# A hybrid diffusion layer on one core: GpSimd's tables, weight splits and key copies on VectorE and ScalarE, and a latent scan in 8 blocks of 4 chunks

## The chip, the cores and the metric

The kernel runs on one core of a Trainium2 chip. The time is the device time of one execution in microseconds (us); less is better. Five engines work beside each other, each through its own queue: TensorE (PE) does the matmuls and transposes, VectorE (DVE), ScalarE (ACT) and GpSimd (POOL) the work on elements, and SyncE (SP) issues the loads from HBM.

## The reference

One layer over 256 latent tokens and 256 context tokens of 1024 channels, batch 1, all in float32:

```
mod  = silu(c) @ w_mod + b_mod                      # six rows: shift, scale, gate, twice
h    = rmsnorm(x) * (1 + scale) + shift             # the same for the context tokens
proj = h @ w_in                                     # S5 input 512 | K 128 | V 128 | Q 512 | gates 2048
y    = S5(proj): 32 groups of 16 channels, 64 complex states, both directions;
       the context's last state is the start of the latent scan
o    = attention of the latents over latents and context (8 query heads, 2 key heads,
       normalised q and k, rotary positions on the latents)
x    = x + gate1 * ((gates_a * glu(gelu(y)) @ w_ssm_out + gates_b * o @ w_attn_out) @ w_out)
h2   = rmsnorm(x) * (1 + scale2) + shift2
x    = x + gate2 * sum over the top 4 of 32 experts: swiglu(h2 @ w_gate_up[e]) @ w_down[e]
out  = rmsnorm(x) * final_norm_g
```

## The kernel before

SBUF is used as 24 pages of 128 x 2048 floats (`pg(i)`, L54). A page is filled by a load, read by matmuls, and given back with `release` (L151) or `used` (L172): this issues the next load of one long list (gates, GLU, output projections, then for each expert eight tiles of w_gate_up and four of w_down, 1 MB each). All loads stand in SyncE's queue in program order (`load`, L89), so that a load that waits for its page holds up those behind it.

The work has two parts. The dense part (to about 380 us in the profile) makes the modulation, the projections, S5, attention and the merge. In the experts' part every expert's weights stream through the pages.

A planner orders each engine's instructions by program order and readiness; only where `strict["on"]` is set are TensorE's instructions pinned to program order (L79 to L86). It is off up to the gate splits and on from there. SyncE's loads are always pinned. VectorE, ScalarE and GpSimd are not pinned in the dense part up to the merge.

S5 is worked in chunks of 8 tokens, 32 chunks for the context and 32 for the latents. `v_tables` (L553) builds for each quarter of the groups a real and an imaginary table from the input matrix and powers of the multiplier, six operations on 128 x 1024 floats; of quarters 0 and 1 the imaginary half runs on GpSimd. `v_transposes` (L574) transposes them on TensorE. `w_tables` (L596) builds the readout tables in the same way, six operations for each of four quarters, all on GpSimd, three quarters ahead of the key and value projections and the last after the transposes of U. `scan_multipliers` (L516) fills the tile `LS` with the multiplier's powers for 1, 2, 4, 8 and 16 chunks by 28 operations on 128 x 32 floats. `chunk_in` and `chunk_T` (L727, L739) give each chunk's own contribution to the state, in `vv[0]` (page 8) for the context and `vv[1]` (page 9) for the latents. `scan_up` (L864) reduces the context to one state `h0` in five levels. `scan_steps` (L877) walks over the latents' chunks one after the other: 31 steps of `cmul_add` (L852), which is four VectorE operations, here on 128 x 64 floats.

`split` (L61) takes a float32 weight apart into a rounded part, copied by ScalarE, and the rest, subtracted by the engine that it is given. `gate_split` (L766) does so for the gate columns, two pieces of 512 columns a call, on GpSimd.

After the gate splits of tile 0 and `scan_up` a loop of 16 steps u runs. Each step has 24 gate matmuls (`gate_mm`, L920, which also splits half of the next gate tile), up to u = 8 a part of the scan, up to u = 7 one group of `k_kernel` (L946), which reads all four W tables, and from u = 4 on a step of attention. After u = 7 the kernels go to HBM (`Rd`), and after `scan_out` at u = 9 `kernel_in` (L1041) loads them back in another layout; the readout follows at u = 11 and 12.

Of the kernel before, what the change touches and what calls it, by code (L numbers as in the profile page):

```python
# [15 lines left out]
AF = mybir.ActivationFunctionType  # L16
# [13 lines left out]
P_QT, P_K, P_M, P_A, P_S, P_RO, P_RT, P_GL, P_B, P_BS, P_BL, P_BP = 1, 0, 10, 4, 9, 11, 13, 15, 1, 3, 1, 3  # L30
# [3 lines left out]
def hybrid_block(ctx: ExitStack, tc: tile.TileContext, a: dict, out: bass.AP):  # L34
    nc = tc.nc
    V, S, G, T = nc.vector, nc.scalar, nc.gpsimd, nc.tensor
# [17 lines left out]
    def pg(i, o=0, n=PW):  # L54
        return pages[i][:, o:o + n]
# [5 lines left out]
    def split(src, hi, lo, eng):  # L61
        S.activation(hi.bitcast(F32R), src, AF.Copy)  # L62
        eng.tensor_sub(lo.bitcast(F32R), src, hi)  # L63
# [63 lines left out]
    stream, loaded, where = [], {}, {}  # L127
# [23 lines left out]
    def release(*ps):  # L151
        for p_ in ps:
            renew(p_)
            j = state["next"]
            state["next"] = j + 1
            if j < len(stream):
                key, src = stream[j]
                k, f = src.shape[1], src.shape[2]
                t = pg(p_, 0, k * f).rearrange("p (k f) -> p k f", k=k)
                if j == len(stream) - 1:  # L160
                    for k in (0, 4):
                        load(t[:, k:k + 4], src[:, k:k + 4])
                else:
                    load(t, src)
                loaded[key], where[key] = t, p_
            elif j == len(stream):
                state["fg"] = p_
                fg_row = pg(p_, 1024, 1024)[0:1]
                load(fg_row, a["final_norm_g"][None, :])
                G.partition_broadcast(pg(p_, 0, 1024), fg_row)  # L170
# [39 lines left out]
    wu = [load_cols(w_in, 0, 512, 22, 0, 4)]  # L210
# [302 lines left out]
    LS = sm([128, 5, 2, 2, 32], "LS")  # L513
# [39 lines left out]
    def v_tables(qt):  # L553
        gs = slice(8 * qt, 8 * qt + 8)
        td = pg(7, 0, 1024).rearrange("p (g t k) -> p g t k", g=8, t=8)

        def bc(r):
            return BB[:, r, gs].unsqueeze(2).to_broadcast([128, 8, 8, 16])

        def lc(r):  # L560
            return LV[:, r, :, gs].rearrange("p t g -> p g t").unsqueeze(3).to_broadcast([128, 8, 8, 16])

        VR, VI = v_part(qt, 0), v_part(qt, 1)
        V.tensor_mul(VR, bc(0), lc(0))
        V.tensor_mul(td, bc(1), lc(1))
        V.tensor_sub(VR, VR, td)
        E2 = V
        if qt < 2:
            E2, td = G, pg(20, 0, 1024).rearrange("p (g t k) -> p g t k", g=8, t=8)
        E2.tensor_mul(VI, bc(0), lc(1))  # L570
        E2.tensor_mul(td, bc(1), lc(0))
        E2.tensor_add(VI, VI, td)  # L572

    def v_transposes(qt):  # L574
        for g2 in range(4):
# [18 lines left out]
    WR, WI = [], []  # L594

    def w_tables(qt):  # L596
        gs = slice(8 * qt, 8 * qt + 8)
        td = pg(20, 1024 * (qt % 2), 1024).rearrange("p (g j k) -> p g j k", g=8, j=8)
        for r, tab in ((0, WR), (1, WI)):
            tab.append(pg((18, 19, 11, 12)[qt], 1024 * r, 1024).rearrange("p (g j k) -> p g j k", g=8, j=8))  # L600

        def cc(r):
            return CT[:, r, gs].unsqueeze(2).to_broadcast([128, 8, 8, 16])

        def lw(r):
            return LW[:, r, :, gs].rearrange("p t g -> p g t").unsqueeze(3).to_broadcast([128, 8, 8, 16])

        G.tensor_mul(WR[qt], cc(0), lw(0))
        G.tensor_mul(td, cc(1), lw(1))
        G.tensor_add(WR[qt], WR[qt], td)  # L610
        G.tensor_mul(WI[qt], cc(1), lw(0))
        G.tensor_mul(td, cc(0), lw(1))
        G.tensor_sub(WI[qt], WI[qt], td)

# [23 lines left out]
    renew(11, "r")  # L640
    wuh, wul = [pg(p_).rearrange("p (k f) -> p k f", k=4) for p_ in (12, 11)]
    for k in range(4):
        split(wu[1][:, k], wuh[:, k], wul[:, k], V if k % 2 else G)
    last = mod0_rows(1)
    del held["m", 0], held["m", 1]
    with tc.issue_after(last.ins):
# [17 lines left out]
    mod_tile()  # L664
    renew(11)
    renew(12)
    for qt in range(3):
        w_tables(qt)
    v_transposes(1)
    v_tables(3)  # L670
    v_transposes(2)
# [26 lines left out]
    for h in range(2):  # L698
        for j4 in range(2):
            b = bank()  # L700
# [10 lines left out]
    for h in range(2):  # L711
        for g4 in range(2):
            b = bank()
# [3 lines left out]
            V.tensor_copy(U[:, 4 * g4:4 * g4 + 4, :, h], b.rearrange("p (g q c) -> p g q c", g=4, q=4))  # L717

    mod_tile()
    w_tables(3)  # L720
    split(wq[1], wqh[1], wql[1], V)
    mod_load(16)

# [15 lines left out]
    def chunk_T(i, vo):  # L739
        b = bank()  # L740
        for j in range(2):
            for r in range(2):
                ttrans(b[:, 128 * (2 * r + j):128 * (2 * r + j) + 128],
                            vo[:, 256 * j + 128 * r:256 * j + 128 * r + 128], ident)
        for h in range(2):
            bv = b.rearrange("p (r g h c) -> p h c r g", r=2, g=4, h=2)[:, h]
            V.tensor_copy(vv[h][0:64, :, :, 4 * i:4 * i + 4], bv[0:64])
            S.activation(vv[h][64:128, :, :, 4 * i:4 * i + 4], bv[64:128, ::-1], AF.Copy)

    prev = None  # L750
    for i in range(8):
# [6 lines left out]
        if i in (2, 4):  # L758
            q_proj(i // 2 - 1)
    chunk_T(7, prev)  # L760
    release(20)
    renew(4)

# [2 lines left out]
    def gate_split(i, j):  # L766
        for k in range(0, 8, GK):
            sl = slice(k, k + GK)
            split(loaded["gate", i][:, sl, 128 * j:128 * j + 128], wgh[:, j, sl], wgl_[:, j, sl], G)


    cosq, sinq = sm([128, 2, 64], "cosq"), sm([128, 2, 64], "sinq")
# [40 lines left out]
    for tt in range(4):  # L813
        kvw = kv_ps[tt // 2].rearrange("p (t h f) -> p t h f", t=2, h=4)[:, tt % 2, 0:2]
        r_k = rsn[:, 16 + 2 * tt:18 + 2 * tt]
        d0 = kn[:, tt, :, 0]
        if tt < 2:
            V.tensor_mul(d0, kvw, kg_row.unsqueeze(1).to_broadcast([128, 2, 64]))
            V.tensor_mul(d0, d0, r_k.unsqueeze(2).to_broadcast([128, 2, 64]))
        else:  # L820
            rope_norm(d0, kvw, cosk[:, tt - 2], sink[:, tt - 2], r_k, 2, d0)
        G.tensor_copy(kn[:, tt, :, 1], d0)


    qs = pg(22).rearrange("p (t h r f) -> p t h r f", r=2, t=2, h=8)
# [26 lines left out]
    def cmul_add(h_out, h_in, v_in, lv, n, t1, t2):  # L852
        lr_ = LS[:, lv, 0].unsqueeze(1).to_broadcast([128, n, 2, 32])
        li_ = LS[:, lv, 1].unsqueeze(1).to_broadcast([128, n, 2, 32])
        V.tensor_mul(t1, h_in, lr_)  # L855
        V.tensor_mul(t2, h_in[:, :, ::-1], li_)
        V.tensor_add(t1, t1, v_in)
        V.tensor_add(h_out, t1, t2)  # L858
# [3 lines left out]
    h0 = LS[:, 4, 0:1]  # L862
# [9 lines left out]
            n //= 2  # L872


    H = [h0] + [vv[1][:, s:s + 1] for s in range(31)]

    def scan_steps(s0, s1):  # L877
        for s in range(s0, s1):
            cmul_add(H[s + 1], H[s], H[s + 1], 0, 1, LS[:, 2, 0:1], LS[:, 3, 0:1])

    Hn = pg(8).rearrange("p (g r c) -> p g r c", g=32, r=2)

# [266 lines left out]
    for u in range(16):  # L1149
        gate_mm(u // 2, u % 2)  # L1150
        if mods["done"] < 16:
            p_ = mod_tile()
            if mods["done"] == 16:
                release(23)
        i = u // 2 + 1
        if u % 2 and i < 8 and not (where["gate", i] == 20 and state["next"] >= 8):
            used("gate", i)
        if u == P_QT:
            for i in range(2):
                q_T(i)  # L1160
                k_T(i)
        if P_K <= u < 8 + P_K:
            k_kernel(u - P_K)
        if u == 7 + P_K:
            Rd = dpool.tile([16, 32, 240], F32, name="Rd")
            for q in range(4):
                for e in range(2):
                    load(Rd[:, 8 * q:8 * q + 8].rearrange("p (g e) m -> p e g m", e=2)[:, e],
                                R[32 * q + 16 * e:32 * q + 16 * e + 16].rearrange("p (g e) m -> p e g m", e=2)[:, e])
        if u == P_M:  # L1170
            mod_rows(1)
            mod_rows(2)
        if u == P_M + 1:
            shift_logits()
        if u >= P_A:
            attn(n_attn)
            n_attn += 1
        if u == P_S:
            scan_out()
            kernel_in()  # L1180
        if u < P_S:
            s1 = 31 * (u + 1) // P_S
            scan_steps(n_scan, s1)
            n_scan = s1
        if u in (P_RO, P_RO + 1):
            readout(u - P_RO)
        if u == P_RO + 1:
            release(18, 19, 11, 12, 9)
            load(n2row, w("norm2_g")[None, :].to_broadcast([128, 1024]))
        if u == P_RT:  # L1190
            readout_T()
            gelu()
        if u == 15:
            wsplit()
            wsplit()
        if u == P_GL:
            glu()
        for n in range(3):
            if u == P_B + P_BS * n:
                bias_load(1024 * n, w("b_gate_up")[:, 1024 * n:1024 * n + 1024] if n < 2 else w("b_down"))  # L1200
            for j in range(2):
                if u == P_B + P_BS * n + P_BL + j:
                    bias_parts(1024 * n, (512 * j,))
# [519 lines left out]
```

## Time and profile before

| | us |
|---|---|
| median of 3 runs | 1323.57 |
| lowest and highest | 1322.31 to 1325.38 |
| the profiled execution | 1321.38 |
| its span, first to last instruction | 1319.7 |

In the span TensorE is busy 1170.8 us, VectorE 439.7, ScalarE 196.5 and GpSimd 158.1. 462.57 MB are moved. The rows below name instructions by the line of the kernel (L522), the engine, and out<-in by tile (`pg` is any page, `bk` a PSUM bank).

### The profile page before, as it was taken

Reading aid. Unit: us, or ns where it says so; the run is one execution under the profiler, and the core shown is the slowest. Engines: PE = TensorE matmul, PEld = TensorE weight load, DVE = VectorE, ACT = ScalarE, POOL = GpSimd, SP = SyncE. Lnnn points to the kernel's source line nnn. Section 1 sums busy time; section 2 is a strip of 40 time slices with the busy share of each in tenths; the row PEclk is TensorE's granted clock in tenths of the full one; section 3 lists DMA queues with packets and bytes.
Section 4 is the critical chain, followed back from the end, with each engine's and each line's share of the span. In section 5 each row is a group of like instructions: output and inputs, shape, how many; then the busy total and the mean of one; then the engine's idle time right before and its main releaser. Section 6 shows DMA issues by size and latency. Waiting matters only on the chain.

```text
span 1319.7 us, 16264 instructions
## 1 busy us (share of the span) xinstructions
PE 1170.8 (89%) x6711; PEld 541.5 (41%) x6712; DVE 439.7 (33%) x929; ACT 196.5 (15%) x368; POOL 158.1 (12%) x115
## 2 busy tenths in 40 slices
PE   4563998689999999999999989999898989899986
PEld 2363666578843333333332323323232323233224
DVE  5999389757331121111221111121111111111111
ACT  3231343654110000000000000000000000000001
POOL 1479563412000000000000000000000000000000
PEclk9876899889999999999999999999999999999998
DMA  9810567777989999999999999999999999999996
GB/s 277 279 33 33 191 233 240 116 219 276 352 337 416 416 417 416 416 418 417 418 418 417 418 417 416 417 416 417 417 418 417 417 417 417 417 417 415 416 392 205
DMA packets 123105, 462.57 MB, mean 351 GB/s; under 512 B 20669, under 2 KB 46953, under 8 KB 88210
## 3 DMA queue, kind: packets, MB, share of 16 engines
q1 hardware_dynamic: 122562, 460.90, 89.7%
q8 instruction: 55, 0.90, 0.3%
q0 software_dynamic: 416, 0.56, 0.1%
q14 instruction: 24, 0.20, 0.0%
q10 hardware_dynamic: 48, 0.01, 0.0%
HBM read 459.89 MB, written 1.54 MB: 350 GB/s over the span
## 4 chain that ended last, share of the span: by engine, by line
PE 49%; DMA 37%; DVE 10%; issue 2%; SPq 1%; ACT 1%; POOL 0%; DVEq 0%; ACTq 0%; POOLq 0%
PE bk L83 46%; DMA pg<-in_w_gate_up_dram 28%; DMA pg<-in_w_down_dram 7%; PE bk L86 3%; DMA pg<-Rd 1%; DVE pg L63 1%; DVE pg L858 1%; SPq L90 1%; DVE LS L528 1%; DVE LS L855 1%; DVE pg L522 0%; DVE LS L523 0%; DVE pg L848 0%; DVE pg L380 0%; DVE LS L529 0%
## 5 line engine op out<-in xcount | busy, mean ns | idle before, releaser
L83 PE MATMUL bk<-pg,pg 128*64 128x512 f32 (+6 forms) x5344 | 995.6, 476 | 65.6 <-DMA pg<-in_w_down_dram 28.3
L83 PEld LDWEIGHTS bk<-pg,pg 128*64 128x64 f32 (+3 forms) x5344 | 448.3, 154 | 552.4 <-issue 351.8
L86 PE MATMUL bk<-ident,pg 128*128 128x128 f32 x480 | 83.0, 301 | 57.3 <-DVE pg L572 21.0
L1460 DVE TENSOR_SCALAR pg<-bk 128x512 f32<-128x512 f32 x32 | 22.1, 692 | 290.7 <-PE bk L83 290.7
L1371 DVE TENSOR_TENSOR pg<-bk,shT 128x512 f32<-128x512 f32 x32 | 22.1, 692 | 266.4 <-PE bk L83 266.4
L86 PEld LDWEIGHTS bk<-ident,pg 128*128 128x128 f32 x480 | 56.6, 150 | 123.0 <-issue 48.1
L1577 POOL DMA_DIRECT2D pg<-g2d x2 | 1.3, 642 | 882.2 <-PE bk L83 882.2
L1493 DVE TENSOR_TENSOR pg<-bk,pg 128x512 f32<-128x512 f32 x30 | 20.8, 692 | 188.8 <-PE bk L83 188.8
L1472 ACT ACTIVATE pg<-bk 128x256 f32<-128x256 f32 x32 | 12.3, 383 | 395.4 <-PE bk L86 395.4
L83 PE MATMUL bk<-pg 64*128 64x512 f32 (+1 forms) x368 | 70.5, 486 | 0.0
L1477 ACT ACTIVATE pg<-bk 128x512 f32<-128x512 f32 x32 | 19.1, 596 | 257.4 <-PE bk L86 257.4
L63 POOL TENSOR_TENSOR pg<-pg,pg 128x512 fp32r<-128x512 f32 x34 | 47.5, 1412 | 43.8 <-ACT pg L62 36.8
L62 ACT ACTIVATE pg<-pg 128x512 fp32r<-128x512 f32 (+3 forms) x63 | 43.7, 721 | 56.8 <-PE bk L83 35.8
L1461 ACT ACTIVATE pg<-pg 128x512 f32<-128x512 f32 x32 | 20.1, 630 | 187.0 <-DVE pg L1460 186.9
L83 PEld LDWEIGHTS bk<-pg 64*128 64x128 f32 (+1 forms) x368 | 20.0, 162 | 50.4 <-issue 50.4
L63 DVE TENSOR_TENSOR pg<-pg,pg 128x512 fp32r<-128x512 f32 (+3 forms) x29 | 33.7, 1176 | 3.3 <-ACT pg L62 2.9
L83 PE MATMUL bk<-pg,selB 128*64 128x512 bf16 (+1 forms) x196 | 34.4, 388 | 0.0
L83 PE MATMUL bk<-pg,scond 128*32 128x256 f32 (+1 forms) x256 | 29.0, 525 | 0.0
L1462 DVE TENSOR_SCALAR pg<-bk 128x512 f32<-128x512 f32 x32 | 22.1, 692 | 5.3 <-PE bk L83 5.3
L1463 DVE TENSOR_TENSOR pg<-pg 128x512 f32<-128x512 f32 x32 | 21.8, 683 | 2.1 <-ACT pg L1461 2.0
L1464 DVE SCALAR_TENSOR_TENSOR pg<-pg 128x512 f32<-128x512 f32 x32 | 22.1, 692 | 1.1
L1468 DVE TENSOR_SCALAR pg<-iot,posp,gate 128x128 f32<-128x128 f32 x64 | 18.9, 340 | 0.0
(301 smaller groups left out, 539.1 us busy)
## 6 DMA issues: line engine op xcount, KB each, us to landing
pg<-in_w_gate_up_dram SPq DMA_DIRECT2D x256, 1024.0 KB, 20.0
pg<-in_w_down_dram SPq DMA_DIRECT2D x127, 1024.0 KB, 20.0
pg<-in_w_mod_dram SPq DMA_DIRECT2D x16, 1024.0 KB, 5.4
pg<-in_w_in_dram SPq DMA_DIRECT2D x13, 1024.0 KB, 9.0
pg<-in_w_mod_dram SPq DMA_DIRECT2D x16, 512.0 KB, 9.1
pg<-in_w_out_dram SPq DMA_DIRECT2D x4, 1024.0 KB, 11.8
pg<-Rd SPq DMA_DIRECT2D x16, 128.0 KB, 8.5
pg<-in_w_ssm_out_dram SPq DMA_DIRECT2D x2, 1024.0 KB
```

Source lines behind the costliest of these rows:

```text
L62: S.activation(hi.bitcast(F32R), src, AF.Copy)
L63: eng.tensor_sub(lo.bitcast(F32R), src, hi)
L83: pinned(T.matmul(*ar, **kw))
L86: pinned(T.transpose(*ar))
L1371: pv_(V.tensor_add(xg[p % 2][:, 4 * half:4 * half + 4], pb.rearrange("p (k m) -> p k m", k=4), shk[:, 4 * half:4 * half + 4].unsqueeze(2). ...
L1460: pv_(V.tensor_scalar(gx, pgate, 7.0, None, op0=ALU.min))
L1461: pa_(S.activation(sx, gx, AF.Sigmoid, scale=1.702))
L1462: pv_(V.tensor_scalar(ux, pup, 7.0, -7.0, op0=ALU.min, op1=ALU.max))
L1463: pv_(V.tensor_mul(gx, gx, sx))
L1464: pv_(V.scalar_tensor_tensor(ux, ux, 1.0, gx, op0=ALU.add, op1=ALU.mult))
L1477: pa_(S.activation(dst, pmx, AF.Copy))
L1493: pv_(V.tensor_mul(yx, pdn, g2h))
```

## The change

The GpSimd operations of `v_tables`, `w_tables`, `gate_split` and of the splits of the S5 input's weights go to VectorE; the four copies of the normalised keys go to ScalarE. The four calls of `w_tables` now stand together behind the last `chunk_T`, and their scratch lies in pages 19, 11, 12 and 3 instead of page 20. GpSimd keeps the rotary tables, memsets, broadcasts and a few loads.

The 31 steps over the latents' chunks become 15 pieces. Three pieces combine, for 8 blocks of 4 chunks at once, the chunks of a block into one sum `Sb`; one copy and seven small steps carry the state over the blocks (`Hb`, with the multiplier's power for four chunks, `LS[:, 2]`); three pieces spread it over the chunks of all blocks at once; one copy sets the last chunk of each block. The big pieces are `cmul_add` on 128 x 512 floats.

```diff
@@ v_tables
-        E2 = V
-        if qt < 2:
-            E2, td = G, pg(20, 0, 1024).rearrange("p (g t k) -> p g t k", g=8, t=8)
-        E2.tensor_mul(VI, bc(0), lc(1))
-        E2.tensor_mul(td, bc(1), lc(0))
-        E2.tensor_add(VI, VI, td)
+        V.tensor_mul(VI, bc(0), lc(1))
+        V.tensor_mul(td, bc(1), lc(0))
+        V.tensor_add(VI, VI, td)
@@ w_tables
-        td = pg(20, 1024 * (qt % 2), 1024).rearrange("p (g j k) -> p g j k", g=8, j=8)
+        td = pg((19, 11, 12, 3)[qt], 0, 1024).rearrange("p (g j k) -> p g j k", g=8, j=8)
...
-        G.tensor_mul(WR[qt], cc(0), lw(0))
-        G.tensor_mul(td, cc(1), lw(1))
-        G.tensor_add(WR[qt], WR[qt], td)
-        G.tensor_mul(WI[qt], cc(1), lw(0))
-        G.tensor_mul(td, cc(0), lw(1))
-        G.tensor_sub(WI[qt], WI[qt], td)
+        V.tensor_mul(WR[qt], cc(0), lw(0))
+        V.tensor_mul(td, cc(1), lw(1))
+        V.tensor_add(WR[qt], WR[qt], td)
+        V.tensor_mul(WI[qt], cc(1), lw(0))
+        V.tensor_mul(td, cc(0), lw(1))
+        V.tensor_sub(WI[qt], WI[qt], td)
@@ the projection of the S5 input
-    split(wu[1][:, k], wuh[:, k], wul[:, k], V if k % 2 else G)
+    split(wu[1][:, k], wuh[:, k], wul[:, k], V)
@@ ahead of the key and value projections
-    for qt in range(3):
-        w_tables(qt)
@@ after the transposes of U
-    w_tables(3)
@@ after the chunks
     chunk_T(7, prev)
+    for qt in range(4):
+        w_tables(qt)
     release(20)
@@ gate_split
-            split(loaded["gate", i][:, sl, 128 * j:128 * j + 128], wgh[:, j, sl], wgl_[:, j, sl], G)
+            split(loaded["gate", i][:, sl, 128 * j:128 * j + 128], wgh[:, j, sl], wgl_[:, j, sl], V)
@@ the keys
-        G.tensor_copy(kn[:, tt, :, 1], d0)
+        S.activation(kn[:, tt, :, 1], d0, AF.Copy)
@@ the scan over the latents' chunks
-    H = [h0] + [vv[1][:, s:s + 1] for s in range(31)]
+    vb = vv[1].rearrange("p (b i) r g -> p i b r g", i=4)
+    Sb, Hb, tb1, tb2 = [pg(8, 512 * i, 512).rearrange("p (s r g) -> p s r g", s=8, r=2) for i in range(4)]
+    def scan_pieces():
+        for i in range(1, 4):
+            yield lambda i=i: cmul_add(Sb, Sb if i > 1 else vb[:, 0], vb[:, i], 0, 8, tb1, tb2)
+        for b in range(8):
+            if b:
+                yield lambda b=b: cmul_add(Hb[:, b:b + 1], Hb[:, b - 1:b], Sb[:, b - 1:b], 2, 1, tb1[:, 0:1], tb2[:, 0:1])
+            else:
+                yield lambda: V.tensor_copy(Hb[:, 0:1], h0)
+        for i in range(3):
+            yield lambda i=i: cmul_add(vb[:, i], vb[:, i - 1] if i else Hb, vb[:, i], 0, 8, tb1, tb2)
+        yield lambda: V.tensor_copy(vb[:, 3, 0:7], Hb[:, 1:8])
+    pieces = list(scan_pieces())
     def scan_steps(s0, s1):
         for s in range(s0, s1):
-            cmul_add(H[s + 1], H[s], H[s + 1], 0, 1, LS[:, 2, 0:1], LS[:, 3, 0:1])
+            pieces[s]()
@@ the loop of 16 steps
-            s1 = 31 * (u + 1) // P_S
+            s1 = len(pieces) * (u + 1) // P_S
```

## Rows read from the trace of the kernel before

**Rows 1.** Experts' part: busy us (instructions) by engine, granted clock, DMA share, GB/s

```profile
860.00:920.00 60.00, 55.61 (x264) 18.61 (x262) 9.57 (x20) 3.22 (x6) 0.00 (x0) 1.00 1.02 417
```

**Rows 2.** The dense part by stretches A to E, the same columns

```profile
50.50:134.00 83.50, 37.16 (x250) 32.74 (x246) 82.39 (x68) 19.88 (x31) 72.27 (x32) 0.70 0.20 56
134.00:183.00 49.00, 48.68 (x363) 32.91 (x364) 25.69 (x61) 18.27 (x37) 24.74 (x18) 0.95 0.59 200
183.00:241.60 58.60, 41.47 (x582) 31.17 (x582) 55.80 (x155) 26.07 (x51) 28.75 (x24) 0.88 0.62 208
241.60:268.50 26.90, 20.09 (x163) 17.70 (x165) 18.32 (x46) 18.15 (x31) 10.37 (x8) 0.88 1.14 172
268.50:380.00 111.50, 111.30 (x893) 93.76 (x895) 57.10 (x114) 36.88 (x78) 13.83 (x12) 0.98 0.77 283
```

**Rows 3.** The chain that ended last: start, length in us, what

```profile
88.78 1.13 DVE pg L564
...
241.68 4.41 DMA Rd<-pg
...
268.45 8.02 PE bk L83 x118
```

**Rows 4.** TensorE's waits in A: us in total, times, longest

```profile
PE bk L86 <- DVE pg L572: 21.0, 2, 16.7
```

**Rows 5.** Timeline of VectorE in A: start, length, line, operation, shapes

```profile
73.58 0.17 DVE L529 TENSOR_SCALAR LS<-LS 128x32 f32<-128x32 f32 x1
...
76.24 2.06 DVE L523 TENSOR_TENSOR LS<-pg 128x32 f32<-128x32 f32 x1
78.22 2.05 DVE L529 TENSOR_SCALAR LS<-LS 128x32 f32<-128x32 f32 x1
```

**Rows 6.** Timeline of GpSimd, the same moments

```profile
75.58 2.68 POOL L608 TENSOR_TENSOR pg<-pg,pg 128x1024 f32<-128x1024 f32 x1 [10.73 <-ACT pg L591]
78.21 2.02 POOL L609 TENSOR_TENSOR pg<-pg,pg 128x1024 f32<-128x1024 f32 x1
```

**Rows 7.** Stretch A, instructions on tile LS alone: VectorE, ScalarE, clock, DMA, GB/s

```profile
50.50:134.00 83.50, 38.75 (x28) 0.00 (x0) 0.70 0.20 56
```

**Rows 8.** VectorE's groups in A: count, busy us, mean ns, idle before

```profile
L63 DVE TENSOR_TENSOR pg<-pg,pg 128x512 fp32r<-128x512 f32 x6 | 7.7, 1340 | 0.2 <-PE bk L83 0.2
...
L380 DVE TENSOR_SCALAR pg<-pg,gsc,shc 128x256 f32<-128x256 f32 x4 | 6.1, 1583 | 0.0
...
L564 DVE TENSOR_TENSOR pg<-pg,pg 128x1024 f32<-128x1024 f32 x4 | 4.8, 1210 | 0.0
...
L572 DVE TENSOR_TENSOR pg<-pg,pg 128x1024 f32<-128x1024 f32 x2 | 4.5, 2228 | 0.0
```

**Rows 9.** Timeline of VectorE while GpSimd stands still

```profile
66.37 2.48 DVE L63 TENSOR_TENSOR pg<-pg,pg 128x512 fp32r<-128x512 f32 x4
```

**Rows 10.** VectorE's groups from 20 to 47 us

```profile
L380 DVE TENSOR_SCALAR pg<-pg,gsc,shc 128x256 f32<-128x256 f32 x4 | 1.4, 407 | 0.1
```

**Rows 11.** VectorE's waits in B: us in total, times, longest

```profile
DVE pg L717 <- PE bk L86: 9.2, 1, 9.2
DVE pg L747 <- PE bk L86: 7.4, 3, 5.6
```

**Rows 12.** VectorE's groups from 180 to 262 us

```profile
L858 DVE TENSOR_TENSOR pg<-LS 128x64 f32<-128x64 f32 x31 | 12.8, 413 | 0.9
L855 DVE TENSOR_TENSOR LS<-pg,LS 128x64 f32<-128x64 f32 x30 | 9.3, 310 | 0.8
...
L857 DVE TENSOR_TENSOR pg<-pg,pg 128x1024 f32<-128x1024 f32 x1 | 2.3, 2289 | 0.0
```

**Rows 13.** Timeline of VectorE in C: one line in two consecutive steps

```profile
205.17 0.23 DVE L855 TENSOR_TENSOR LS<-pg,LS 128x64 f32<-128x64 f32 x1
...
205.96 0.22 DVE L855 TENSOR_TENSOR LS<-pg,LS 128x64 f32<-128x64 f32 x1
```

**Rows 14.** Stretch C, line 63 alone: VectorE, GpSimd, clock, DMA, GB/s

```profile
183.00:241.60 58.60, 2.97 (x4) 24.30 (x16) 0.88 0.62 208
```

## Predicting the time

> **What bounds the kernel now.** I read the stretches by stage first. In the experts' part (a stretch of 60 us stands for it) the DMA engines show a share of 1.02 at 417 GB/s, while TensorE has gaps [rows 1]: the end of the kernel is set by when that stream of weights begins to run without a gap, about 380 us, plus bytes that the change doesn't touch. Those loads start when pages come free, and pages come free as the dense part advances. So what the dense part loses or gains before 380 us moves the end by as much. In the dense part five stretches have different limits [rows 2]. A (50.5 to 134 us): VectorE is busy 82.4 of 83.5 us, TensorE 37.2 at a granted clock of 0.70, a mean between its two levels of 1.2 and 2.4 GHz. B (134 to 183): TensorE 48.7 of 49, VectorE 25.7. C (to 241.6): VectorE 55.8 of 58.6, TensorE 41.5. D (to 268.5): the kernels' round trip through HBM, from the store of Rd to the first readout matmul [rows 3]. E (to 380): TensorE without a gap. The chain of waits says the same: TensorE's longest wait in A, 16.7 us, is for VectorE's line 572 [rows 4].
>
> Then I asked why VectorE is so busy in A. Its timeline shows operations on 32 columns that take 2.05 us, where the same line took 0.17 us just before [rows 5]. GpSimd's timeline beside it shows its 1024-column operations starting and ending at the same moments: 75.58 plus 2.68 is 78.26, and VectorE's L523 ends at 78.30; GpSimd's next ends at 80.23, VectorE's L529 at 80.27 [rows 5, 6]. The two engines take turns, one operation each, however small VectorE's is. What that costs in A: the 28 small operations that fill the tile LS take 38.75 us there [rows 7]. So the bound in A is not VectorE's work but its turns with GpSimd.
>
> **The change, part by part.** Free costs come from rows without GpSimd beside them: 0.17 us for 32 columns [rows 5]; 1.21 us for 1024 columns [rows 8], of which the chain of waits counts 1.13 before the next one starts [rows 3]; 0.62 us for 512 (four in 2.48 us) [rows 9]; 0.41 us for 256 columns of tensor_scalar [rows 10].
>
> *A.* Gone: the 28 small ones, 38.8 to 28 x 0.17 = 4.8, so -34.0 [rows 7]. The six 512-column splits, 7.7 to 3.7: -4.0. L380, 6.1 to 1.6: -4.5. L572, 4.5 to 2.4: -2.1 [rows 8]. That is -44.6. Added: the imaginary half of the first two V tables, 6 x 1.21 = 7.3, and two weight splits, 1.2. VectorE in A goes from 82.4 to 46.3 us, and A could shorten by 37. I take 33: TensorE's 37.2 us of matmuls in A depend back and forth on these tables, and GpSimd keeps the small rope tables, so some 4 us of new gaps are likely. What is late next in A is TensorE itself: by its busy time A can't be under 37 us at the low clock, which isn't far below VectorE's 46.
>
> *B.* The four W tables are 24 operations of 1024 columns with the same broadcasts as L564. No row shows them on VectorE. The lower bound is 24 x 1.13 = 27, the upper one GpSimd's own undisturbed 2.02 us each [rows 6], 48; the nearest row is L564, and I take 28. They stand behind the chunks in the program, but nothing pins VectorE's order there, so a planner may put them earlier where their operands are ready. VectorE has 23 us idle in B, mostly waiting for TensorE's transposes: 9.2 us before L717 and 7.4 us before L747 [rows 11]. Four gate splits also come to B, 2.5. So 28 + 2.5 - 23 = 7 to 8 us stick out at B's end, the more so as the last table must wait until the chunks have read page 3. I take +8. If nothing of it is covered it costs 28. Who waits: the first k_kernel matmuls in TensorE's pinned order, which need all four tables; behind them the whole loop of 16 steps.
>
> *C.* Turns with GpSimd again: L858 averages 413 ns and L855 310 ns [rows 12] where a free one takes 0.23 us [rows 13]: 31 x 0.18 + 30 x 0.08 = 8. In the context scan a 1024-column L857 took 2.29 us instead of 1.21 [rows 12], and a handful like it make about 4 us in all (an estimate from that row). The new scan: a free step of the old one takes 0.79 us (from one L855 to the next) [rows 13], 31 steps 24.5. The new one has 6 operations of four instructions on 512 columns, 24 x 0.62 = 14.9, seven small steps, 5.5, and two copies of about 0.5: 21.4, so -3. The blocks alone are thus worth little. Against it come the gate splits: 16 of them lie in C, 24.3 us on GpSimd [rows 14]; on VectorE 16 x 0.62 = +10. They stand in VectorE's queue between softmax and scan; behind them wait the gate matmuls two steps later and SyncE's next page release, so a late one is covered by one loop step. Sum of C: -8 - 4 - 3 + 10 = -5.
>
> *The key copies* go to ScalarE: four of 128 columns. No row shows them there; about 0.5 us each as the mean of ScalarE's 37 instructions in B (18.3 us, of 49 us) [rows 2]. They can only matter where the transposes of k wait for them, 0 to 2 us; I take 0.
>
> *D and E.* D is DMA latency from the last kernel row, not changed. In E TensorE has no gap; the last twelve or so splits land on a VectorE that is half idle there [rows 2], so 0. The DMA share in A to D is between 0.20 and 1.14, the latter only in D; 31 MB in 218 us leave room for an earlier release of pages.
>
> **Sum.** -33 + 8 - 5 = -30 us at the first readout matmul, and the same at the end. The profiled execution took 1321.4 us (span 1319.7); the median of the runs is 2.2 us above it. 1321.4 - 30 + 2.2 gives about 1293.
>
> **The rivals.**
> 1. *The W tables are not covered.* If they run as one block between the chunks and the loop, the 28 us go onto the path instead of 8, and the gain shrinks to 10 or 13: 1310. For it: their place in the program, page 3, and a VectorE that has no idle time left from 168 us on. Against it: 23 idle us in B and two tables whose pages are free early. One rule of the Trainium skill points this way: "Perfetto Trace Analysis", section Optimizing Scalar/DVE Operations, says that GpSimd and VectorE share a read port, so that moving work between the two may not help. The turns show the sharing [rows 5, 6]; by the rule alone the gain would be only the difference of the two engines' times for an operation, 2.0 less 1.1, some 25 us for 30 operations, or about 1298. Chance 0.20.
> 2. *More than I count.* No gaps in A (-37), B's surplus only 2, C at -10 because part of the splits and the scan falls behind the last kernel row: -45, and 1279. VectorE's total before the last kernel row (46 in A, 26 + 2.5 + 28 in B, 51 in C: 153 of the 191 us that the three now take) forbids much more, some 38 with nothing moved behind that row. For it: TensorE's clock of 0.70 in A would rise with fewer gaps. Chance 0.13.
> 3. *Slower: the 2 us operations are not turns with GpSimd* but something of VectorE's own, such as its small operations in that place. Then A gains nothing and VectorE gets all the new work: +8.5 in A, +8 in B, +10 - 3 in C, so +23, about 1347. It decides from the moment at which VectorE's rows of 32 columns stay at 2 us with GpSimd idle. Against it: the equal ends [rows 5, 6] and the 0.17 us of the same line. Chance 0.05.
> 4. *It doesn't reach the end.* The dense part shortens, but the expert stream starts as before, because a page that it needs is still released late: 1323. Against it: after 380 us every load waits for TensorE's progress or for the queue. Chance 0.04.
>
> **How the numbers follow.** Forecast 1293 (its own range 1284 to 1303) with chance 0.58; the rivals as above. The range for 8 in 10 takes in rivals 1 and 2: 1277 to 1312. About 0.2%, 2.6 us, is what a measurement of this kernel can tell from no change. Faster by more: 0.58 + 0.20 + 0.13 = 0.91, rounded down to 0.90; within: 0.04; slower: 0.06.
>
> **What would show it.** In the changed profile VectorE's L523 to L529 at 0.17 us and TensorE's 16.7 us wait gone: step A right. W table operations inside VectorE's waits for transposes: step B right; as a block ahead of the first k_kernel matmul with TensorE idle: rival 1. The new scan's 512-column rows at 0.62 us. Expert stream at 417 GB/s without a gap from about 350 us. Wrong would be the whole if stretched VectorE rows remain with GpSimd idle, or if TensorE's pinned order meets a new long wait in the loop.

## The result and the profile after

The changed kernel takes 1283.82 us (median of 4 runs, 1282.83 to 1285.06) against 1323.14 before (four runs, one more than in the table above): a ratio of 0.9701, with a 95% interval of 0.9684 to 0.9718. That is 39 us less, where 30 were forecast: just below the forecast's own range of 1284 to 1303, and inside the wider one of 1277 to 1312. The profiled execution took 1285.06 us with a span of 1283.4; its span is 36.3 us shorter than that of before. The 3 us between the two differences are run to run: the profiled execution of before lies 1.8 us below its median, that of after 1.2 above.

The same five stretches can be found in every kernel by four marks: the end of the last V table operation (end of A), the first k_kernel matmul (end of B), the last row of the kernels on VectorE (end of C) and the first readout matmul (end of D). Read from the timelines, in us from the span's start:

| | A ends | B ends | C ends | D ends | span |
|---|---|---|---|---|---|
| before | 130.6 | 179.4 | 241.6 | 268.45 | 1319.7 |
| after | 96.2 | 153.8 | 201.7 | 230.3 | 1283.4 |
| change of the stretch | -34.4 | +8.8 | -14.3 | +1.7 | +1.8 (from D to the end) |

So the gain is made in A and C, B gives some back, and the rest moves as a block. These are the stretches of after between its marks; the columns are those of [rows 2].

```profile
50.50:96.20 45.70, 33.78 (x258) 28.26 (x250) 44.35 (x76) 17.43 (x28) 17.27 (x7) 0.92 0.44 131
96.20:153.80 57.60, 45.98 (x292) 31.52 (x292) 53.91 (x91) 22.97 (x47) 4.17 (x6) 0.89 0.40 144
153.80:201.70 47.90, 43.31 (x660) 33.55 (x657) 46.40 (x108) 24.50 (x45) 1.89 (x2) 0.96 0.79 260
201.70:230.30 28.60, 19.50 (x154) 17.16 (x153) 21.68 (x43) 18.46 (x33) 1.32 (x3) 0.86 1.15 159
```

In A VectorE is still busy all the time, 44.35 of 45.7 us, but the stretch is not much over half as long, and TensorE's granted clock is 0.92 instead of 0.70 [rows 2]. In B VectorE, idle for half of it before, is busy 53.9 of 57.6 us. The small operations that fill LS, 38.75 us in [rows 7], now take 5.09 (busy time of the operations on LS in A, the columns as above without the engines that have none):

```profile
50.50:96.20 45.70, 5.09 (x28) 0.00 (x0) 0.92 0.44 131
```

VectorE's timeline (start and duration in us) has L523 and L529 at 0.17 to 0.18 us, where [rows 5] has 2.05:

```profile
75.06 0.17 DVE L529 TENSOR_SCALAR LS<-LS 128x32 f32<-128x32 f32 x1
...
77.66 0.18 DVE L523 TENSOR_TENSOR LS<-pg 128x32 f32<-128x32 f32 x1
77.76 0.17 DVE L529 TENSOR_SCALAR LS<-LS 128x32 f32<-128x32 f32 x1
```

The W tables (lines 605 to 610 of the changed kernel) don't run where they are called. The first runs right behind the last V table at 97 us, ahead of the chunks, and the others between the copies of B:

```profile
94.98 1.21 DVE L569 TENSOR_TENSOR pg<-pg,pg 128x1024 f32<-128x1024 f32 x1
96.11 1.28 DVE L699 COPY pg<-bk 128x512 f32<-128x512 f32 x2
97.31 1.21 DVE L605 TENSOR_TENSOR pg<-pg,pg 128x1024 f32<-128x1024 f32 x1
98.44 1.21 DVE L606 TENSOR_TENSOR pg<-pg,pg 128x1024 f32<-128x1024 f32 x1
...
110.51 1.21 DVE L610 TENSOR_TENSOR pg<-pg,pg 128x1024 f32<-128x1024 f32 x1
111.64 0.74 DVE L741 COPY pg<-bk 64x256 f32<-64x256 f32 x2
112.31 1.21 DVE L605 TENSOR_TENSOR pg<-pg,pg 128x1024 f32<-128x1024 f32 x1
...
137.26 1.20 DVE L610 TENSOR_TENSOR pg<-pg,pg 128x1024 f32<-128x1024 f32 x1
```

TensorE's waits in the dense part (us in total, times, longest) have changed their kind. The 16.7 us of [rows 4] are gone. The longest is now for the first gate split, which stands behind the W tables and the rotary work in VectorE's queue:

```profile
PE bk L83 <- DVE pg L63: 11.6, 2, 10.2
PE bk L83 <- DMA pg<-Rd: 7.7, 1, 7.7
PE bk L86 <- DVE pg L367: 3.0, 1, 3.0
```

The expert stream reaches its rate at 340 us, where the kernel before reaches it at 380, some 40 us earlier, and from there on both run alike [rows 1]. The slice of before that opens the stream has the same count of 76 matmuls, 16.74 us of them and a granted clock of 0.91 as the slice of after that opens it (before in the first fence, after in the second):

```profile
380.00:400.00 20.00, 16.74 (x76) 5.62 (x74) 5.71 (x20) 4.14 (x6) 0.00 (x0) 0.91 1.00 415
```
```profile
340.00:360.00 20.00, 16.74 (x76) 5.61 (x74) 5.71 (x20) 4.14 (x6) 0.00 (x0) 0.91 1.00 407
360.00:380.00 20.00, 20.00 (x108) 8.79 (x106) 4.66 (x8) 2.30 (x3) 0.00 (x0) 1.00 1.01 413
860.00:920.00 60.00, 55.84 (x264) 18.95 (x264) 10.02 (x20) 3.22 (x6) 0.00 (x0) 1.00 1.02 417
```

### The profile page after: what moved, and what is told of

It reads as the page before. It is cut to its first block, busy times and chain, and to the rows that moved or that the text cites. A ratio compares the mean times of both kernels' runs of the same rounds, so it can differ in the third digit from the quotient of the medians.

```text
span 1283.4 us, 16161 instructions
## 1 busy us (share of the span) xinstructions
PE 1167.6 (91%) x6711; PEld 538.0 (42%) x6712; DVE 424.4 (33%) x923; ACT 197.3 (15%) x372; POOL 39.1 (3%) x47
## 4 chain that ended last, share of the span: by engine, by line
PE 44%; DMA 43%; DVE 9%; issue 2%; SPq 1%; ACT 1%; POOL 0%; DVEq 0%; POOLq 0%; ACTq 0%
PE bk L83 41%; DMA pg<-in_w_gate_up_dram 30%; DMA pg<-in_w_down_dram 11%; PE bk L86 3%; DVE pg L63 2%; DMA pg<-Rd 2%; SPq L90 1%; DVE pg L853 0%; DVE pg L851 0%; DVE pg L854 0%; DVE pg L565 0%; DVE pg L568 0%; DVE pg L566 0%; DVE pg L564 0%; DVE pg L844 0%
## 5 line engine op out<-in xcount | busy, mean ns | idle before, releaser
L86 PE MATMUL bk<-ident,pg 128*128 128x128 f32 x480 | 79.9, 292 | 18.6 <-DVE pg L367 4.2
L63 DVE TENSOR_TENSOR pg<-pg,pg 128x512 fp32r<-128x512 f32 (+3 forms) x63 | 50.6, 817 | 18.4 <-ACT pg L62 16.3
L1373 DVE TENSOR_SCALAR pg<-iot,posp,rs 128x64 f32<-128x64 f32 x64 | 15.7, 306 | 0.1
```

What stands on the lines that cost most here:

```text
L86: pinned(T.transpose(*ar))
```

## Experiments

Two theories had to be told apart from others. The first: VectorE loses time because it takes turns with GpSimd, and the moves pay because that ends. The second: as long as VectorE is full from A to C, its sum sets the end, and neither the blocks of the scan nor TensorE's own waits do. All times are medians beside runs of the kernel before on the same chip (1324.4 to 1324.9 us there); ratios are to those, with 95% intervals. Where a run is compared with the changed kernel, two figures mean the difference by the ratios and by the medians.

**The blocks of the scan, alone and taken back.** `e1_blocks_alone` is the kernel before with the 15 pieces in place of the 31 steps; `e2_steps_back` is the changed kernel with the 31 steps.

```diff
-            cmul_add(H[s + 1], H[s], H[s + 1], 0, 1, LS[:, 2, 0:1], LS[:, 3, 0:1])
+            pieces[s]()
```

> The kernel before with only the latents' scan in 8 blocks; all GpSimd work stays. My theory (turns with GpSimd are what VectorE loses; the blocks themselves save 24.5 - 21.4 = 3 us of VectorE, and fewer small operations wait behind GpSimd's 16 splits): 1315 to 1320. Rival (the blocks carry the gain, the moves only cost): 1295 or less.

> The changed kernel with the old 31 steps. My theory: with GpSimd idle a step takes 0.79 us, so the old scan costs about 3 us more of VectorE's time ahead of the last kernel row: 1284 to 1290. Rival (the blocks carry the gain): 1310 or more.

Measured: e1 1323.63 us, ratio 0.9986 (0.9975 to 0.9997); e2 1285.22 us, ratio 0.9696 (0.9678 to 0.9715), not to be told from the changed kernel's 0.9701. The blocks are worth 0 to 3 us. e1 lies above the 1315 to 1320 that I had expected, since I thought that fewer small operations would wait behind GpSimd and save more. Its stretch C, from its first k_kernel matmul to its last kernel row, says why not:

```profile
180.10:242.10 62.00, 47.89 (x668) 37.38 (x665) 60.04 (x110) 26.45 (x49) 32.10 (x22) 0.89 0.65 223
```

VectorE runs 110 instructions there where before ran 165 in the same stretch (62.2 us), and it is as busy, 60.0 us. What VectorE loses goes by the number of GpSimd's operations, not of its own: with fewer and longer ones each GpSimd operation still takes its turn.

**The W tables alone, and their place alone.** `e3_w_tables_alone` is the kernel before with only the W tables on VectorE, called behind the chunks. `e4_place_alone` calls them there too, but leaves them on GpSimd.

```diff
-        G.tensor_mul(WR[qt], cc(0), lw(0))
+        V.tensor_mul(WR[qt], cc(0), lw(0))
...
     chunk_T(7, prev)
+    for qt in range(4):
+        w_tables(qt)
```

> The kernel before with only the four W tables on VectorE behind the chunks; V tables, splits, key copies and scan as before. My theory: stretch A loses its turns with 18 of GpSimd's 1024-column operations, about -30, B grows by about 6, C stays: 1296 to 1303. Rival (the two engines share a port, so moving work between them doesn't help): 1318 or more.

> The kernel before with the four W tables still on GpSimd but called behind the chunks, with the new scratch pages. My theory: the place in the program binds only a busy queue; GpSimd is idle, so the planner starts them as early as before and the turns stay: 1318 to 1330. Rival (the place behind the chunks is what frees A): A is as short as in the changed kernel, 24 operations of 2 us on GpSimd in B and C: under 1310.

Measured: e3 1299.24 us, ratio 0.9803 (0.978 to 0.9827); e4 1315.99 us, ratio 0.9927 (0.9907 to 0.9947). e3 is inside its expectation: A ends at 98.3, B at 154.1, C at 219.6 us. So 32 of A's 34 us come from the W tables leaving GpSimd, and C is not shorter at all without the other moves (65.5 us). Moving these 24 operations from one engine to the other gives 25 us, so the rival (it doesn't help) falls. e4 lies between its two expectations, and mine is 2 us off: A ends at 120.6, 10 us earlier than before. GpSimd's timeline shows the step that I had wrong:

```profile
89.23 3.13 POOL L612 TENSOR_TENSOR pg<-pg,pg 128x1024 f32<-128x1024 f32 x1
92.32 0.45 POOL L774 TENSOR_TENSOR cosq<-pg,qg_row 128x128 f32<-128x128 f32 x1
92.73 3.45 POOL L613 TENSOR_TENSOR pg<-pg,pg 128x1024 f32<-128x1024 f32 x1
...
119.62 2.88 POOL L608 TENSOR_TENSOR pg<-pg,pg 128x1024 f32<-128x1024 f32 x1
136.20 2.03 POOL L609 TENSOR_TENSOR pg<-pg,pg 128x1024 f32<-128x1024 f32 x1 [13.70 <-PE bk L86]
```

GpSimd isn't idle in A but full, so the place bound there too: the small rotary tables now come ahead (L774 at 92 us), and ten of the 24 operations wait until after 136 us and run in B, beside a VectorE that has time. In A there are 14 of them, where before had 19: fewer turns, a shorter A.

**Work on GpSimd that nobody needs.** To the changed kernel come operations in page 20, which is free in A, whose values nothing reads: 18 additions of two inputs in `e8_idle_gpsimd_work`, 36 copies of one input in `e10_gpsimd_copies`.

```diff
     renew(12)
+    for n in range(18):
+        G.tensor_add(pg(20, 0, 1024), pg(20, 0, 1024), pg(20, 1024, 1024))
     v_transposes(1)
```

```diff
     renew(12)
+    for n in range(36):
+        G.tensor_copy(pg(20, 0, 1024), pg(20, 1024, 1024))
     v_transposes(1)
```

> The changed kernel with 18 additions of 1024 columns on GpSimd in stretch A, in page 20, whose values nothing reads. If VectorE takes turns with them, it loses up to 18 x 2.0 = 36 us in A, and its operations on 32 columns take 2 us again: 1305 to 1320. If the stretched operations before had another cause: 1284 to 1287.

> The changed kernel with 36 copies of 1024 columns on GpSimd in stretch A in page 20, one input each, whose values nothing reads. If any GpSimd operation that reads SBUF holds VectorE off, A grows by about GpSimd's busy time for them (each some 1 us, so 30 us or more): 1305 to 1325. If only operations with two inputs do: 1283 to 1290.

Measured: e8 1319.28 us, ratio 0.9961 (0.9947 to 0.9975), nearly the whole gain lost; e10 1309.56 us, ratio 0.9884 (0.9862 to 0.9906). In e8 A ends at 132.1 instead of 96.2 us: 35.9 us for 18 operations, which is 18 x 2.0, GpSimd's time for such an operation in [rows 6]. The first fence is a line of GpSimd's timeline, where the 18 operations stand, the second VectorE's beside it:

```profile
49.56 49.23 POOL L665 TENSOR_TENSOR pg<-pg 128x1024 f32<-128x1024 f32 x18 [33.62 <-PE bk L83]
```
```profile
53.21 10.06 DVE L63 TENSOR_TENSOR pg<-pg,pg 128x512 fp32r<-128x512 f32 x4 [3.38 <-PE bk L83]
63.19 0.41 DVE L367 COPY pg<-bk 128x256 f32<-128x256 f32 x1
...
65.41 0.15 DVE L376 SCALAR_TENSOR_TENSOR gsc<-bk,cols 128x4 f32<-128x4 f32 x1
65.59 2.32 DVE L378 TENSOR_TENSOR gsc<-gsc,cols 128x4 f32<-128x4 f32 x1
67.94 9.78 DVE L380 TENSOR_SCALAR pg<-pg,gsc,shc 128x256 f32<-128x256 f32 x4
```

Four splits take 10.06 us, where the changed kernel needs 2.50 for them. L378 on four columns with both inputs in SBUF takes 2.32 us; L376 beside it, which reads PSUM, 0.15, and the copy L367 out of PSUM 0.41 as ever. The copies of e10 with one input hold VectorE as well, only for less, being shorter (1.04 us undisturbed): A ends at 122.4 us, 26 us later for 36 of them, which take GpSimd 37 us without waits.

```profile
71.50 2.05 DVE L565 TENSOR_TENSOR pg<-pg,pg 128x1024 f32<-128x1024 f32 x1
73.47 2.05 DVE L567 TENSOR_TENSOR pg<-pg,pg 128x1024 f32<-128x1024 f32 x1
75.45 2.05 DVE L566 TENSOR_TENSOR pg<-pg,pg 128x1024 f32<-128x1024 f32 x1
```

These are VectorE's 1024-column operations, 1.21 us in [rows 8], at 2.05. The turns are shown directly: work without any user costs what the W tables cost. Not all work on GpSimd does: its memset of 128 x 1024 in the changed kernel (0.96 us from 129.31), which reads nothing, lies beside a 1024-column VectorE operation that took 1.21 us as ever (L608 at 129.36).

**The gate splits back on GpSimd.** `e5_gate_splits_back` is the changed kernel with one letter changed.

```diff
-            split(loaded["gate", i][:, sl, 128 * j:128 * j + 128], wgh[:, j, sl], wgl_[:, j, sl], V)
+            split(loaded["gate", i][:, sl, 128 * j:128 * j + 128], wgh[:, j, sl], wgl_[:, j, sl], G)
```

> The changed kernel with the gate splits' subtraction back on GpSimd, 1.27 us each. My prediction's sums: on VectorE the 16 splits in C cost 10 us and save about 12 us of turns, so 1284 to 1290. Rival (the splits on VectorE are a net loss since they make TensorE wait 10.2 us for the first one): 1275 to 1280.

Measured: 1293.12 us, ratio 0.9757 (0.9741 to 0.9773), 7 to 9 us more than the changed kernel and 3 beyond what I expected. Its stretches B and C:

```profile
97.00:150.90 53.90, 46.17 (x292) 31.20 (x292) 50.13 (x67) 20.70 (x41) 13.60 (x12) 0.91 0.51 175
150.90:211.40 60.50, 45.94 (x654) 35.41 (x651) 59.61 (x116) 26.28 (x52) 27.89 (x19) 0.87 0.60 197
```

C is 60.5 us long, nearly the 62.2 of before, and VectorE is busy for all of it although 14 splits fewer are its own than in the changed kernel. Comparing each of its VectorE rows with the same line and shape in the changed kernel, 4.4 us are stretched in B and 12.5 in C: 17 us of turns for 20 splits. On VectorE those splits cost 20 x 0.6 = 12. That explains 5 us of the difference. Which of VectorE's other work falls ahead of the last kernel row may change with it, but that isn't shown, and I can't split the rest further.

**The W tables on VectorE at their old places.** `e6_old_place`:

```diff
+    for qt in range(3):
+        w_tables(qt)
     v_transposes(1)
...
+    w_tables(3)
     split(wq[1], wqh[1], wql[1], V)
...
     chunk_T(7, prev)
-    for qt in range(4):
-        w_tables(qt)
```

> The changed kernel with the W tables on VectorE at their old places: three ahead of the key and value projections, one after the transposes of U, scratch in page 20 as before. My theory: VectorE is full in A, so there the place binds; A gets about 20 us longer and 15 to 23 idle us in B aren't filled: 1297 to 1305. Rival (VectorE's total alone counts, the place doesn't): 1282 to 1287.

Measured: 1295.33 us, ratio 0.9772 (0.9755 to 0.9788). A ends at 115.8 us, 20 later, as expected; B is 44.9 us instead of 57.6, C 53.8 instead of 47.9. The place is worth 9 to 11 us on VectorE: it decides how much of the W tables fills B's gaps. That is a little less than expected.

**TensorE's longest wait.** `e11_first_split_early` puts the first gate tile's splits ahead of the rotary work.

```diff
+    gate_split(0, 0)
+    gate_split(0, 1)
     cosq, sinq = sm([128, 2, 64], "cosq"), sm([128, 2, 64], "sinq")
...
-    gate_split(0, 0)
-    gate_split(0, 1)
     used("gate", 0)
```

> The changed kernel with the first gate tile's splits ahead of the rotary work in VectorE's queue; TensorE waits 10.2 us for the first of them in the changed kernel. My theory: VectorE's sum is the bound, so an earlier start of the loop's first matmuls only moves TensorE's wait to the next thing that VectorE owes it: 1282 to 1286. Rival (that wait is on the path by itself): 1274 to 1278.

Measured: 1285.92 us, ratio 0.9705 (0.9685 to 0.9725): no change. TensorE's 10.2 us for that split are 2.6, and it waits elsewhere in their place:

```profile
PE bk L83 <- DMA pg<-Rd: 8.2, 1, 8.2
PE bk L86 <- DVE pg L917: 6.9, 1, 6.9
PE bk L83 <- DVE pg L816: 3.1, 1, 3.1
PE bk L86 <- DVE pg L367: 3.0, 1, 3.0
PE bk L83 <- ACT pg L62: 2.7, 1, 2.7
PE bk L83 <- DVE pg L63: 2.6, 1, 2.6
```

The first k_kernel matmul comes 5 us earlier (148.8), the last kernel row 0.8 us later (202.4). B ends earlier and nothing is won: VectorE's sum decides.

**Less for VectorE.** `e7_copies_scalar` gives the eight copies of 128 x 512 out of PSUM for A and U to ScalarE; `e9_more_copies_scalar` also the lower halves of the chunks' transposes, 16 copies of 64 x 256.

```diff
-            V.tensor_copy(A[:, h, :, 4 * j4:4 * j4 + 4],
-                          b.rearrange("p (j g k) -> p g j k", j=4, g=8))
+            S.activation(A[:, h, :, 4 * j4:4 * j4 + 4],
+                         b.rearrange("p (j g k) -> p g j k", j=4, g=8), AF.Copy)
```

```diff
-            V.tensor_copy(vv[h][0:64, :, :, 4 * i:4 * i + 4], bv[0:64])
+            S.activation(vv[h][0:64, :, :, 4 * i:4 * i + 4], bv[0:64], AF.Copy)
```

> The changed kernel with the eight copies of 128x512 out of PSUM for A and U on ScalarE in place of VectorE. My theory: VectorE is what A to C wait for, and 8 x 0.6 = 4.8 us leave it: 1279 to 1283. Rival (they lie in TensorE's waits for transposes anyway): 1283 to 1286.

> The changed kernel with the copies for A and U on ScalarE and also the chunk transposes' lower halves (16 copies of 64x256 out of PSUM, 0.41 us each on VectorE). My theory: VectorE's sum from A to C is the bound as long as it is full there, so another 16 x 0.34 to 0.41 = 5.5 to 6.5 us go: 1272 to 1277. Rival (ScalarE or TensorE's transposes take over in B): 1278 to 1282.

Measured: e7 1279.77 us, ratio 0.9676 (0.965 to 0.9702), 3 to 4 us below the changed kernel, though the two intervals overlap; e9 1273.85 us, ratio 0.9616 (0.9599 to 0.9633), 10 to 11 us below the changed kernel and clear of it. For 4.8 and some 11 us taken from VectorE the kernel gives back 3 to 4 and 10 to 11. Busy time in three stretches of e9 (the same columns):

```profile
96.00:150.00 54.00, 49.42 (x363) 33.11 (x361) 52.03 (x79) 33.26 (x73) 4.17 (x6) 0.94 0.60 207
150.00:200.00 50.00, 45.08 (x616) 36.68 (x617) 48.72 (x117) 26.46 (x50) 2.90 (x4) 0.93 0.77 242
```

VectorE is still full; TensorE has 49.4 of 54 us from 96 to 150 us, so in B the next engine is near.

## Why the prediction was right, and where it was short

**What bounds the kernel.** Right. What the dense part gains comes out at the end nearly whole: 38.1 us at the first readout matmul, 36.3 at the end of the profiled execution, and the expert stream begins some 40 us earlier and runs alike from then on. Rival 4 (it doesn't reach the end) falls.

**A.** Forecast -33, measured -34.4. The small operations on LS were put at 4.8 us and take 5.09. VectorE's whole was put at 46.3 us and is 44.35. Of the rivals, the third (the 2 us are VectorE's own) falls twice: the same instructions take 0.17 us when GpSimd is idle, and e8 brings stretched rows back by GpSimd work alone. e3 shows that the W tables make A's gain, and the V tables and the two weight splits only some 2 us of it. The prediction's floor of 37 us for A was TensorE's busy time at a mean clock of 0.70, 37.2 us for 250 matmuls. After, 258 matmuls took 33.8 us at 0.92, so TensorE was further from being the limit than the prediction had it.

**B.** Forecast +8, measured +8.8. The cover is the one named: VectorE's idle time in B falls from 23.3 us (48.8 less 25.5) to 3.7, filled by W table operations between the copies. Rival 1 (one block of 28 us) doesn't occur. e6, with the tables called at their old places, leaves VectorE 14.4 us idle in B and is 9 to 11 us slower, so the cover comes from the place.

**C.** Forecast -5, measured -14.3; here lies nearly the whole miss. As work crosses the marks, B and C are best taken together: VectorE's time is its own work, its turns, and its idle time.

| B and C, VectorE | forecast | measured |
|---|---|---|
| own work | +28 + 12.5 - 3 = +37.5 | +31.1 (69.2 to 100.3) |
| turns with GpSimd | -12 | -15.7 |
| idle | -23 | -20.9 (26.1 to 5.2) |
| sum | +3 (rounded) | -5.5 (111.0 to 105.5) |

The turns are each VectorE row's length over that of the same line and shape in the changed kernel, 1.9 us in B and 13.8 in C (good to about 1 us, by how the overlap of neighbouring rows is counted); own work is busy time less these. The forecast had counted the steps of the scan and a handful of rows of the context scan, and no others. The own work grew less than counted because some of it left the two stretches: the split of the first half of the query weights, 2.2 us, and two of the four copies for A, 0.6 each, ran at the start of B before (from 131 us) and run in A now (from 89 us). That is 3.4 of the 6 us; the W tables, at 1.13 us each 27.2 instead of 28, are another 0.8, and the rest isn't found. The terms were the right ones, three of them wrong in size, two of them to the same side. At the first readout matmul the misses add up to some 8 us: 9.3 in C and 1.4 in A, less 0.8 in B and 1.7 in D.

**The blocks.** Forecast -3 us of VectorE's time in C, with the remark that they are worth little alone. e1 and e2 agree: 0 to 3 us.

**The gate splits and the key copies.** The forecast had the gate splits on VectorE gain a little (12 us of turns against 10 of work in C); e5 puts them at 7 to 9 us, as even the 20 splits in B and C cost 17 us of turns. The key copies take 0.30 us each on ScalarE, where 0.5 was estimated; no run moves them alone, so what they are worth isn't shown.

**D and E.** Forecast 0, measured +1.7 and +1.8 us in the one execution profiled, which is as much as the profiled execution differs from its median.

**The rule quoted from the Trainium skill** ("Perfetto Trace Analysis", section Optimizing Scalar/DVE Operations), that moving work between the two engines might not help, comes to 1298 by the prediction's working. The product there, 30 operations of 0.9 us, is 27 and not 25, so it should be 1296 or 1297. The change gained 39 us, more than that. e3, which moves only the W tables, is at 1299.24, but not for the rule's reason: the W tables' difference per operation doesn't enter, since on VectorE they fill time in B that was idle. That the two numbers are close is chance.

**Rival 2 (more than I count, 1279).** The result lies between it and the forecast. Its C, 10 us shorter, came about and more (14.3); its A without gaps (-37) and its surplus of only 2 us in B did not. TensorE's clock in A did rise, from 0.70 to 0.92.

**A sign of being wrong that did appear.** TensorE's pinned order met a new long wait, 10.2 us for the first gate split. e11 shows that it costs nothing: without it TensorE waits for VectorE elsewhere.

## What to carry to other kernels

If operations of a few columns take as long on VectorE as GpSimd's big ones beside them, and end with them, what GpSimd's work costs VectorE comes near to the time that GpSimd alone would need for it, whether or not anything uses it: here 36 of 36 us for 18 additions, 26 of 37 for 36 copies, 17 of 25 for 20 splits. Count then what each operation takes on either engine, and where the full engine has idle time that the planner can fill; the place in the program matters only on an engine that is full. Ahead of a saturated engine it didn't pay here to reorder what waits for it (e11) or to cut its instructions into fewer of the same work (e1); taking work away did, nearly one for one (e7, e9).

## What the runs showed of the hardware

Not expected was that the loss doesn't go by the number of VectorE's own operations: 165 or 110 instructions in C lose about the same (13.8 and 14.5 us) beside GpSimd's 31.0 and 32.1 us. VectorE operations that read PSUM did not wait (0.15 and 0.41 us beside GpSimd's additions), those that read only SBUF did, even with four columns (2.32 us). GpSimd operations with one input hold VectorE too (2.05 us for 1.21, 26 us for 36 copies); a memset, which reads nothing, did not (1.21 us beside it, in the one place looked at).
